# Gate and up projections of a feed-forward stage by one level of Strassen's algorithm

## The chip, the cores and the metric

The kernel runs on one core of one Trainium2 chip. The metric is device time in microseconds (us) of one execution; the kernel before took 2920.21 us (median of 3 runs, 2919.99 to 2921.68). Engines are named as in the profile: PE multiplies matrices (PEld is its loading of stationary operands), DVE and ACT work on vectors, POOL does small things, SP issues all DMAs of this kernel, in one queue that goes in order.

## The reference

One layer of a hybrid network over 16 learned tokens and 2048 tokens of width 1024 in float32: a token mixer (a state space model and a chunked mLSTM, merged by gates, then a projection and a norm), and behind it the channel mixer, which the change is about:

```python
def channel_mixer(x, g_pre, g_post, w_gate, w_up, w_conv, b_conv, w_down):
    h = rmsnorm(x, g_pre)
    a = causal_dwconv(h @ w_gate, w_conv, b_conv)      # 3 taps over the tokens
    y = (jax.nn.gelu(a, approximate=True) * (h @ w_up)) @ w_down
    return x + rmsnorm(y, g_post)
```

w_gate and w_up are 1024 × 2816, w_down is 2816 × 1024. The first 16 tokens give no output; of them only the last two matter here, for the convolution.

## The kernel before

Every float32 product is made of three matmuls in a reduced type: an operand is split into a high part (a copy by ACT, rounded to that type) and a low part (operand minus high part, by DVE), and `mm3` (lines 145 to 148) adds high × high, high × low and low × high. So an operand that is made on the chip costs one operation of ACT and one of DVE beside what makes it.

The order of the instructions on each engine is not written by hand. The program states them in its own order, and a planner sorts them at compile time: on each engine it takes, of what is ready by its own estimate of times, what the program states first. On the chip each engine then keeps that order. A tile of a pool has a tag and a number of buffers; the next tile of a tag waits until the buffer that it takes is no longer read. A pool that is opened where another was closed waits, tile by tile, for those that lay at its place. PSUM has two buffers of tag "mm", four of "ac" and two of "tp", a bank each.

Stages up to line 829 (projections, state space model, mLSTM) are the same in both kernels. What follows:

- Phase C (lines 831 to 1065) goes over four blocks of 512 tokens (the first has 514, with the two tokens ahead). For each block `front_a` and `front_b` fetch the two branches' inputs, `glu` gates the first, `branches` projects and merges both into `mh`, `ml` (high and low part, from pool `cr`), `out_proj` multiplies by `w_out` in two halves of its columns, loading each 128 × 512 slice when it is due, and `out_post` applies the norm and the residual and stores `h1_d` in DRAM. `out_post` of a block is stated behind `branches` of the next one; that of block 3 comes last. Operand tiles `t4(i)` are 128 × 4 × 514 in size; the tags t0 to t7 are in use.
- `norm_tile` (lines 107 to 125) loads 128 tokens of `h1_d`, takes the sum of squares (ACT), the factor (DVE, POOL), scales by it and by the row `g_ffn_pre` (DVE, line 114), transposes by PE (line 120), and splits from PSUM into the FFN's operands (ACT line 124, DVE line 125). Blocks 0 and 1 are done during the last block of phase C into t0 to t7, blocks 2 and 3 at the beginning of the next stage into the tiles q0 to q7.
- The gate and up stage goes over 22 slices m of 128 columns of `w_gate` and `w_up`. `load_w` (lines 137 to 143) fetches each slice of 128 × 1024 and splits it. `ffn_unit` (lines 1090 to 1116) then does a block of tokens: 24 matmuls for gate into "ac" (48 in block 0, whose 514 columns are cut at 258 and 256), a copy to `gp_` (ACT, line 1099), the convolution (ACT line 1106, two taps on DVE line 1108), the function gelu (ACT line 1109), 24 matmuls for up into "mm", the product (DVE, line 1115) and the store to `y_d` (line 1116). All four blocks' operands lie on the chip, so each weight is loaded and split once. The last two columns of a block's gate are kept in `halo` (POOL, lines 1101 and 1104).
- The down stage (lines 1136 to 1183) loads `w_down` in two halves of columns and splits it into t0 to t7 and q0 to q2, and goes twice over 16 tiles of tokens: load `y_d` (line 1160), split (lines 1163 and 1164), 66 matmuls, and the norm and the residual at the end of the second half.

## Time and profile before

| | |
|---|---|
| time, median of 3 runs | 2920.21 us (2919.99 to 2921.68) |
| span of the profiled execution, first to last instruction | 2927.4 us |
| mean granted clock of PE | 0.997 |
| PE busy, matmuls | 2883.3 us (98%), 14862 |
| PEld, loads of stationary operands | 2529.4 us (86%) |
| DVE, ACT, POOL busy | 1346.9 us (46%), 898.9 us (31%), 153.8 us (5%) |
| gate and up stage, first matmul to the down stage | 1444.2 to 2429 us |
| bytes read from and written to DRAM | 244.08 MB, 95.72 MB |

The profiled execution has no separate time of its own beside its span; the span is 7.2 us longer than the median of the runs, which were not profiled. Lines are those of the kernel's file; a helper's line stands for all its callers, so `mm3`'s lines 146 to 148 hold nearly all matmuls, and their output and input tiles tell the stages apart: "ac<-t,wh" and "mm<-q,wh" are the gate and up stage, "ac<-t,yh" the down stage. In rows of groups the numbers are the busy time, the mean length of one in ns, and the idle time of the engine just ahead, with what ended it. In the order of time a row begins with its start and its length; "x2" merges two. Neighbouring instructions of an engine overlap a little in the records, so the cost of one in a row of many is the step from start to start.

### The profile page before, as it was taken

Reading aid. Unit: us, or ns where it says so; the run is one execution under the profiler, and the core shown is the slowest. Engines: PE = TensorE matmul, PEld = TensorE weight load, DVE = VectorE, ACT = ScalarE, POOL = GpSimd, SP = SyncE. Lnnn points to the kernel's source line nnn. Section 1 sums busy time; section 2 is a strip of 40 time slices with the busy share of each in tenths; the row PEclk is TensorE's granted clock in tenths of the full one; section 3 lists DMA queues with packets and bytes.
Section 4 is the critical chain, followed back from the end, with each engine's and each line's share of the span. In section 5 each row is a group of like instructions: output and inputs, shape, how many; then the busy total and the mean of one; then the engine's idle time right before and its main releaser. Section 6 shows DMA issues by size and latency. Waiting matters only on the chain.

```text
span 2927.4 us, 38298 instructions
## 1 busy us (share of the span) xinstructions
PE 2883.3 (98%) x14862; PEld 2529.4 (86%) x14862; DVE 1346.9 (46%) x2617; ACT 898.9 (31%) x1683; POOL 153.8 (5%) x331
## 2 busy tenths in 40 slices
PE   9999999999999999999999999999999999999999
PEld 8999999999999987777788888888888888887887
DVE  4638897377554546566652222222222233224333
ACT  6102232233443435435342222222222232223221
POOL 1000000000000000320310000000000000000000
PEclk9999999999999999999999999999999999999999
DMA  9334453222553655665631111111111134334654
GB/s 298 103 73 139 164 168 114 69 69 71 163 154 119 198 169 159 188 207 165 202 109 44 54 40 51 55 46 54 48 43 54 44 107 126 97 99 145 184 165 124
DMA packets 299848, 342.32 MB, mean 117 GB/s; under 512 B 38849, under 2 KB 208470, under 8 KB 299538
## 3 DMA queue, kind: packets, MB, share of 16 engines
q1 hardware_dynamic: 299666, 339.88, 37.9%
q8 instruction: 116, 1.90, 0.3%
q14 instruction: 66, 0.54, 0.1%
HBM read 244.08 MB, written 95.72 MB: 116 GB/s over the span
## 4 chain that ended last, share of the span: by engine, by line
PE 86%; DMA 5%; DVE 3%; issue 3%; ACT 1%; POOL 1%; SPq 0%; POOLq 0%; DVEq 0%; ACTq 0%
PE mm L146 14%; PE mm L148 14%; PE mm L147 14%; PE ac L146 13%; PE ac L148 13%; PE ac L147 13%; DMA xt<-in_x_dram 1%; DMA wo_d<-W 1%; POOL o L1003 1%; DMA ws<-in_w_out_dram 1%; DMA xs<-in_h_t_dram 1%; PE ac L484 0%; PE ac L482 0%; PE ac L457 0%; PE ac L388 0%
## 5 line engine op out<-in xcount | busy, mean ns | idle before, releaser
L148 PE MATMUL mm<-hTh,wl 128*128 128x410 f32 (+3 forms) x1216 | 430.3, 354 | 0.0
L146 PE MATMUL mm<-hTh,wh 128*128 128x410 f32 (+3 forms) x1216 | 429.6, 353 | 0.2 <-DVE ev L336 0.2
L147 PE MATMUL mm<-hTl,wh 128*128 128x410 f32 (+3 forms) x1216 | 426.7, 351 | 0.0
L130 ACT ACTIVATE wh<-ws 128x512 fp32r<-128x512 f32 (+1 forms) x220 | 171.4, 779 | 478.3 <-PE mm L147 152.4
L1108 DVE SCALAR_TENSOR_TENSOR cc<-gp,cw,cc 128x512 f32<-128x512 f32 x176 | 132.3, 752 | 353.1 <-ACT cc L1106 350.1
L132 DVE TENSOR_TENSOR wl<-ws,wh 128x512 fp32r<-128x512 f32 (+1 forms) x156 | 157.8, 1012 | 243.6 <-ACT wh L130 241.2
L1164 DVE TENSOR_TENSOR yl<-ys,yh 128x1408 fp32r<-128x1408 f32 x64 | 104.0, 1626 | 304.2 <-ACT yh L1163 304.2
L146 PEld LDWEIGHTS mm<-hTh,wh 128*128 128x128 f32 x1216 | 229.4, 189 | 2.9 <-DVE ev L336 0.7
L148 PEld LDWEIGHTS mm<-hTh,wl 128*128 128x128 f32 x1216 | 229.4, 189 | 2.5
L147 PEld LDWEIGHTS mm<-hTl,wh 128*128 128x128 f32 x1216 | 229.4, 189 | 2.1
L147 PE MATMUL ac<-t,wh 128*128 128x512 f32 (+2 forms) x688 | 223.1, 326 | 0.0
L148 PE MATMUL ac<-t,wl 128*128 128x512 f32 (+2 forms) x688 | 220.8, 327 | 1.6 <-DVE wl L134 1.6
L146 PE MATMUL ac<-t,wh 128*128 128x512 f32 (+2 forms) x688 | 222.2, 327 | 0.0
L146 PE MATMUL mm<-t,wh 128*128 128x512 f32 (+2 forms) x544 | 208.1, 383 | 1.8 <-ACT wh L130 1.8
L148 PE MATMUL mm<-t,wl 128*128 128x512 f32 (+2 forms) x544 | 207.1, 383 | 0.7 <-DVE wl L134 0.7
L147 PE MATMUL mm<-t,wh 128*128 128x512 f32 (+2 forms) x544 | 207.2, 381 | 0.0
L146 PE MATMUL ac<-t,yh 128*128 128x512 f32 x512 | 201.8, 394 | 1.4 <-ACT t L1154 0.8
L148 PE MATMUL ac<-t,yl 128*128 128x512 f32 x512 | 202.1, 395 | 0.2 <-DVE yl L1164 0.2
L147 PE MATMUL ac<-t,yh 128*128 128x512 f32 x512 | 202.1, 395 | 0.0
L1163 ACT ACTIVATE yh<-ys 128x1408 fp32r<-128x1408 f32 x64 | 88.4, 1381 | 349.0 <-PE ac L147 347.4
L1099 ACT ACTIVATE gp<-ac 128x512 f32<-128x512 f32 (+2 forms) x110 | 56.0, 510 | 389.9 <-PE ac L148 389.7
L1115 DVE TENSOR_TENSOR cc<-cc,mm 128x512 f32<-128x512 f32 x88 | 60.5, 688 | 189.9 <-PE mm L148 189.7
(425 smaller groups left out, 5806.1 us busy)
## 6 DMA issues: line engine op xcount, KB each, us to landing
ys<-y_d SPq DMA_DIRECT2D x64, 704.0 KB, 4.9
y_d<-cc SPq DMA_DIRECT2D x88, 256.0 KB, 2.0
gab_d<-ev SPq DMA_DIRECT2D x80, 205.0 KB, 2.5
ws<-in_w_m_dram SPq DMA_DIRECT2D x32, 512.0 KB, 3.9
ws<-in_w_out_dram SPq DMA_DIRECT2D x64, 256.0 KB, 3.4
gat<-gab_d SPq DMA_DIRECT2D x48, 256.0 KB, 3.5
ws<-in_w_gate_dram SPq DMA_DIRECT2D x22, 512.0 KB, 3.7
ws<-in_w_up_dram SPq DMA_DIRECT2D x22, 512.0 KB, 3.8
```

The costliest lines, as they stand in the source:

```text
L130: S.activation(wh, ws, AF.Copy, scale=scale)
L132: V.tensor_tensor(wl, ws, wh.bitcast(F32), ALU.subtract)
L146: T.matmul(out=ps, lhsT=lh, rhs=rh, start=first, stop=False)
L147: T.matmul(out=ps, lhsT=lh, rhs=rl, start=False, stop=False)
L148: T.matmul(out=ps, lhsT=ll, rhs=rh, start=False, stop=last)
L1003: (V if b == 3 else G).tensor_tensor(o[:rows], o[:rows], xt[:rows], ALU.add)
L1099: S.activation(gp_[:, o:o + pn], ps, AF.Copy)
L1108: V.scalar_tensor_tensor(c, gp_[:, j:j + 512], cw[:, m, j:j + 1], c, ALU.mult, ALU.add)
L1115: V.tensor_tensor(c, c, pu, ALU.mult)
L1163: S.activation(yh, ys, AF.Copy)
L1164: V.tensor_tensor(yl, ys, yh.bitcast(F32), ALU.subtract)
```

## The change

The gate and up stage becomes a block product: the weights are a 2 × 2 matrix A of blocks (rows gate and up, columns the two halves of the 1024 input features), the normed input is a 2 × 2 matrix B (rows the halves of the features, columns two stretches of tokens). Strassen's algorithm (in Winograd's form) makes the four blocks of A·B from 7 block products instead of 8, with sums of blocks as operands. Two passes over all 22 slices are made: pass 0 over the first 1026 tokens (two stretches of 514 columns, the first beginning with two columns of zeros; each product is cut into 258 and 256 columns), pass 1 over the other 1024 (512 each, not cut). Weights are loaded, summed and split in each pass (`ffn_weights`), with one copy per product.

In `ffn_unit` three PSUM banks A, B, C take the products in the order 1, 6, 2, 7, 5, 4, 3 (A: 1, 2; B: 6, 7, 4; C: 5, 3); a bank is added to by a later product after the sum so far has been read (`mm3x`). Copies to `u1` and of gate's first half are ACT's, the five other sums are DVE's.

The operands from the input are sums too, so `norm_tile` now stores the transposed, normed input as `h2_d` in DRAM (scaled there by `g3`, a column of g_ffn_pre), and `op_load` reads it back, a quarter of a pass at a time, for `ops_first` (operands of products 1, 6, 2, 7) and `ops_second` (5, 4, 3). Their tiles are t0 to t11 and q0, q1, which hold one pass. `ops_first(0)` is stated ahead of `out_post` of block 3, `ops_second(0)` behind it; the norms of blocks 2 and 3 are stated behind slice 1 of pass 0, and the operands of pass 1 between the passes.

To make room, `mh` and `ml` of phase C move to t8 to t11, a pool `mk` of three tiles replaces those of `front_a`, and serves the norm, `op_load` and at the end two of the down stage's tiles. The down stage's pool `el` is opened at the place of `dx`, the gate and up stage's pool, after that is closed; w_down's slices and two small tiles use buffers of the weights' pool `dw`. Removed comments are left out below.

```diff
+    h2_d = dp.tile([128, KD, L], F32, name="h2_d")
...
+    g3 = const.tile([128, KD], F32, name="g3")
+    P.dma_start(out=g3, in_=g_ffn_pre)
+
+    def norm_tile(t, pl, t0, rows):
+
+        xt, hs = t[:, 0:D], t[:, D:2 * D]
+        P.dma_start(out=xt[:rows], in_=h1_d[t0:t0 + rows, :])
         ssq = pl.tile([128, 1], F32, tag="ssq", name="ssq")
         S.activation(hs[:rows], xt[:rows], AF.Square, accum_out=ssq[:rows])
         rs = rstd_of(pl, ssq, rows, 1, 1.0 / D)
-        V.scalar_tensor_tensor(hs[:rows], xt[:rows], rs[:rows], g_b[:rows], ALU.mult, ALU.mult)
+        V.tensor_scalar(hs[:rows], xt[:rows], rs[:rows], None, ALU.mult)
+        hr = xt.rearrange("p (k t) -> p k t", k=KD)
...
-            for j in range(0, per, 4):
-                dh = dst_h[(q * per + j) // 4][:, :, c0:c0 + rows]
-                dl = dst_l[(q * per + j) // 4][:, :, c0:c0 + rows]
-                S.activation(dh, tp[:, j:j + 4], AF.Copy)
-                V.tensor_tensor(dl, tp[:, j:j + 4], dh.bitcast(F32), ALU.subtract)
+            ks = slice(q * per, q * per + per)
+            V.tensor_tensor(hr[:, ks, :rows], tp, g3[:, ks].unsqueeze(2).to_broadcast([128, per, rows]), ALU.mult)
+        P.dma_start(out=h2_d[:, :, t0:t0 + rows], in_=hr[:, :, :rows])
...
+    def mk_tile(dt=F32):
+        return mk.tile([128, 4 * 520], dt, tag="mk", name="mk", bufs=3)
...
-        mh = cr.tile([128, KD, 514], F32R, tag="mh", name="mh")
-        ml = cr.tile([128, KD, 514], F32R, tag="ml", name="ml")
+        mh, ml = [t4(8), t4(9)], [t4(10), t4(11)]
...
+    WX = (514, 512)
+
+    def op_load(p, hf, half):
+        w = WX[p]
+        t = mk_tile()[:, 0:4 * w].rearrange("p (k c) -> p k c", k=2)
+        ks = slice(4 * half + 2 * hf, 4 * half + 2 * hf + 2)
+        if p == 0:
+            G.memset(t[:, :, 0:2], 0.0)
+            P.dma_start(out=t[:, :, 2:2 * w], in_=h2_d[:, ks, 14:14 + 2 * w - 2])
+        else:
+            P.dma_start(out=t, in_=h2_d[:, ks, 1040:1040 + 2 * w])
+        return t[:, :, 0:w], t[:, :, w:2 * w]
+
+    def op_split(op, p, hf, src):
+        hi, lo = (o[:, 2 * hf:2 * hf + 2, 0:WX[p]] for o in op)
+        S.activation(hi, src, AF.Copy)
+        V.tensor_tensor(lo, src, hi.bitcast(F32), ALU.subtract)
+
+    def ops_first(p):
+
+        op = {n: (t4(2 * i), t4(2 * i + 1)) for i, n in enumerate((1, 6, 2, 7))}
+        for hf in range(2):
+            b11, b12 = op_load(p, hf, 0)
+            op_split(op[1], p, hf, b11)
+            b21, b22 = op_load(p, hf, 1)
+            V.tensor_tensor(b11, b12, b11, ALU.subtract)
+            V.tensor_tensor(b12, b22, b12, ALU.subtract)
+            V.tensor_tensor(b22, b22, b11, ALU.subtract)
+            op_split(op[6], p, hf, b22)
+            op_split(op[2], p, hf, b21)
+            op_split(op[7], p, hf, b12)
+        return op
+
+    def ops_second(p, op, last):
+
+        op.update({5: (t4(8), t4(9)), 4: (t4(10), t4(11)), 3: last()})
+        for hf in range(2):
+            b11, b12 = op_load(p, hf, 0)
+            b21, b22 = op_load(p, hf, 1)
+            V.tensor_tensor(b11, b12, b11, ALU.subtract)
+            op_split(op[5], p, hf, b11)
+            V.tensor_tensor(b12, b22, b11, ALU.subtract)
+            V.tensor_tensor(b21, b21, b12, ALU.subtract)
+            op_split(op[4], p, hf, b21)
+            op_split(op[3], p, hf, b22)
...
+    op0 = ops_first(0)
     for f in posts(3):
         f()
     phC.close()
...
+        def put(n, pl, tag, src):
+            t = pl.tile([128, 2, 512], F32R, tag=tag, name=f"w{n}")
+            S.activation(t[:, 0], src, AF.Copy)
+            V.tensor_tensor(t[:, 1], src, t[:, 0].bitcast(F32), ALU.subtract)
+            out_[n] = t.rearrange("p a (k f) -> p a k f", k=4)
...
+        put(1, dw, "wh", a11)
+        V.tensor_tensor(s1, a21, a22, ALU.add)
+        V.tensor_tensor(s2, s1, a11, ALU.subtract)
+        put(6, dw, "wh", s2)
+        put(2, dw, "wl", a12)
+        V.tensor_tensor(s3, a11, a21, ALU.subtract)
+        put(7, dw, "wl", s3)
+        put(5, dx, "w5", s1)
+        put(4, dx, "w4", a22)
+        s4 = dx.tile([128, 512], F32, tag="s3", name="s4")
+        V.tensor_tensor(s4, a12, s2, ALU.subtract)
+        put(3, dx, "w3", s4)
+        return out_
...
+    def ffn_unit(p, m, op):
+        wt = ffn_weights(m)
+        w = WX[p]
+        gp_ = dx.tile([128, 1028], F32, tag="gp", name="gp")
...
+        for p0, pn in (((0, 258), (258, 256)) if p == 0 else ((0, 512),)):
+
+            def prod(ps, n, first):
+                for k in range(4):
+                    mm3x(ps, wt[n][:, 0, k], wt[n][:, 1, k], op[n][0][:, k, p0:p0 + pn], op[n][1][:, k, p0:p0 + pn],
+                         first and k == 0, k == 3)
...
+            A, B, C = pst("ac", [128, pn]), pst("mm", [128, pn]), pst("ac", [128, pn])
+            u1, u2, u3 = acc("u1", 2), acc("u2", 1), acc("u3", 2)
+            prod(A, 1, True)
+            S.activation(u1, A, AF.Copy)
+            prod(B, 6, True)
+            V.tensor_tensor(u2, B, u1, ALU.add)
+            prod(A, 2, False)
+            S.activation(gp_[:, x0 + p0:x0 + p0 + pn], A, AF.Copy)
+            prod(B, 7, False)
+            V.tensor_tensor(u3, B, u1, ALU.add)
+            prod(C, 5, True)
+            V.tensor_tensor(u3, C, u3, ALU.add)
+            prod(B, 4, False)
+            V.tensor_tensor(u1, B, u1, ALU.add)
+            prod(C, 3, False)
+            V.tensor_tensor(gp_[:, x0 + w + p0:x0 + w + p0 + pn], C, u2, ALU.add)
...
+    ops_second(0, op0, lambda: (q4(0), q4(1)))
+    for m in range(NF):
+        ffn_unit(0, m, op0)
+        if m == 1:
+            norm_block(2, dsm)
+            norm_block(3, dsm)
+    op1 = ops_first(1)
+    ops_second(1, op1, lambda: (q4(0), q4(1)))
+    for m in range(NF):
+        ffn_unit(1, m, op1)
+    phX.close()
     el = pool(ctx, "el", bufs=2)
...
-            w_s = el.tile([128, 2, 512], F32, tag="wds", name="wds")
+            w_s = dw.tile([128, 2, 512], F32, tag="wh", name="wds")
```

The rest of the new `ffn_unit` is the convolution, gelu, product and store as before, in two parts of some 512 tokens.

More of the change, by code (lines that the diff above doesn't have):

```diff
@@ L1073, in q4 @@
     def q4(i):
[L1074 to L1081 removed]
+        return hq.tile([128, 4, 514], F32R, tag=f"q{i}", name=f"q{i}")
+    phX = ExitStack()
+    dx = pool(phX, "dx")
+    dsm = Small(dx, "n", 2)
```

158 lines of the change are left out of this document (62 added, 96 removed).

## The prediction

> **What bounds the kernel now.** I read the page's shares first, then the stretches around the stage that changes, then that stage's instructions in order of time.
>
> ```profile
> PE 2883.3 (98%) x14862; PEld 2529.4 (86%) x14862; DVE 1346.9 (46%) x2617; ACT 898.9 (31%) x1683; POOL 153.8 (5%) x331
> PE 86%; DMA 5%; DVE 3%; issue 3%; ACT 1%; POOL 1%; SPq 0%; POOLq 0%; DVEq 0%; ACTq 0%
> ```
>
> PE is busy 98% of the span and holds 86% of the chain that ended last. A busy PE can hide slow matmuls, so the windows come next (after the stretch and its length: PE, PEld, DVE, ACT, POOL busy with their counts, granted clock, DMA share, GB/s).
>
> ```profile
> core 0: us, PE busy (x) PEld busy (x) DVE busy (x) ACT busy (x) POOL busy (x), PEclk, DMA share, GB/s
> 1390.00:1444.00 54.00, 49.34 (x221) 38.80 (x220) 28.93 (x47) 18.74 (x33) 16.33 (x12) 1.00 0.61 190
> 1444.00:1463.00 19.00, 19.00 (x106) 16.49 (x105) 15.33 (x31) 8.78 (x22) 5.63 (x6) 1.00 0.71 231
> 1463.00:1503.00 40.00, 40.00 (x222) 34.15 (x221) 27.46 (x39) 23.10 (x41) 6.45 (x14) 1.00 0.43 148
> 1503.00:2430.00 927.00, 925.93 (x4495) 777.05 (x4494) 249.41 (x317) 229.32 (x335) 24.00 (x124) 1.00 0.18 57
> ```
>
> The gate and up stage runs from 1444 to 2430. PE waits about 1 us in it, at full clock, and DVE works 27% of the time: the stage is as long as its matmuls. Its period per slice m is the distance between two loads of a gate weight; the pitch of matmuls comes from their starts.
>
> ```profile
> 1893.69 0.33 SPq L139 DMA_DIRECT2D ws<-in_w_gate_dram  x1
> 1938.07 0.33 SPq L139 DMA_DIRECT2D ws<-in_w_gate_dram  x1
> 1982.45 0.33 SPq L139 DMA_DIRECT2D ws<-in_w_gate_dram  x1
> ...
> 1444.23 0.28 PE L146 MATMUL ac<-t,wh 128*128 128x258 f32 x1
> 1445.91 0.28 PE L148 MATMUL ac<-t,wl 128*128 128x258 f32 x1
> ...
> 1599.81 0.39 PE L147 MATMUL ac<-t,wh 128*128 128x512 f32 x1
> 1608.38 0.39 PE L148 MATMUL mm<-t,wl 128*128 128x512 f32 x1
> ```
>
> A slice takes 44.38 us: 48 matmuls of 258 or 256 columns and 168 of 512. The 14 steps from 1444.23 to 1445.91 give 0.120 us for 258 columns; I use 0.119 for the mean of 258 and 256. The 37 steps from 1599.81 to 1608.38 give 0.2316 us for 512. Two half-width matmuls cost 0.238, 3% more than one full one.
>
> **The matmuls removed.** For 1024 tokens a slice had 8 products of 4 k tiles (gate and up, two halves of k, two halves of the tokens); now it has 7, each with 4 × 3 = 12 matmuls. Pass 0 cuts all of them at 258 and 256 columns: 168 × 0.119 = 20.0 us. Pass 1 keeps 512: 84 × 0.2316 = 19.45 us. 22 × 39.45 = 868 us against 22 × 44.38 = 976.4: **−108.5 us**. PE needs no further instruction: the transposes of the norm were there before.
>
> **What a slice now asks of DVE and ACT.** The nearest rows:
>
> ```profile
> 1394.85 0.69 DVE L951 TENSOR_TENSOR gat<-gat 128x512 f32<-128x512 f32 x1
> 1395.45 0.69 DVE L132 TENSOR_TENSOR wl<-ws,wh 128x512 fp32r<-128x512 f32 x1
> ...
> 1893.83 1.54 DVE L1108 SCALAR_TENSOR_TENSOR cc<-gp,cw,cc 128x512 f32<-128x512 f32 x2 [0.16 <-ACT cc L1106]
> ...
> L393 DVE TENSOR_TENSOR a<-ac,cc x32: 404/422/430, 334.1 to 488.1; 128x258 f32<-128x258 f32 x32
> ...
> L130 ACT ACTIVATE wh<-ws 128x512 fp32r<-128x512 f32 x78 | 49.3, 632 | 100.8 <-DMA ws<-in_w_out_dram 54.5 <-PE ac L148 22.6 <-DMA ws<-in_w_a_dram 7.5
> L1099 ACT ACTIVATE gp<-ac 128x258 f32<-128x258 f32 x22 | 8.5, 385 | 52.2 <-PE ac L148 52.2
> L1106 ACT ACTIVATE cc<-gp,cb,cw 128x512 f32<-128x512 f32 x88 | 71.8, 816 | 6.1 <-issue 0.4
> L1109 ACT ACTIVATE cc<-cc 128x512 f32<-128x512 f32 x88 | 55.6, 632 | 136.0 <-DVE cc L1108 136.0
> ```
>
> Back to back, a 512-wide two-input operation costs DVE 0.60 us (0.69 long, the next one starts 0.09 before its end); one of 258 from PSUM 0.42 − 0.09 = 0.33; a pair of convolution taps 1.54. Per slice and pass the weights ask for 11 subtractions and additions, since both passes split them anew: 6.6 us. Pass 0 adds 10 sums out of PSUM (3.3), two pairs of taps (3.1) and four products with up (1.3): 14.3 of 20.0 us. Pass 1: 6.6 + 5 × 0.60 + 3.1 + 2 × 0.60 = 13.9 of 19.45. ACT has at most 7 × 0.63 + 4 × 0.39 + 2 × 0.82 + 2 × 0.63 = 8.9 us. So DVE goes from 27% to some 72%: on average it stays behind PE. The 1 MB of weights per slice and pass fits into 20 us (512 KB land in 3.7 us, a row quoted further down).
>
> The **new wait** is inside a slice: the second product into bank A, the second and third into B and the second into C add to a sum that ACT or DVE must have read first, with one other product between. That product lasts 12 × 0.119 = 1.43 us in pass 0 and 2.78 in pass 1.
>
> ```profile
> 1900.09 0.40 PE L148 MATMUL ac<-t,wl 128*128 128x258 f32 x2
> 1900.40 0.39 ACT L1099 ACTIVATE gp<-ac 128x258 f32<-128x258 f32 x1 [2.51 <-PE ac L148]
> ```
>
> The second of these two matmuls starts near 1900.21 and its slot ends at 1900.33; ACT starts 0.07 later. With 0.42 for the reading, 0.5 of 1.43 us is used, so one tap (0.77) ahead in DVE's queue still fits and a pair does not. The taps of slice m−1 and leftovers of the weights of m stand ahead of the sums of m only near a slice's start. Bounds: 0, and 22 slices × 8 reuses × 0.2 = 35. I take 0.3 us a slice: **+7**. Pass 1 has twice the room: 0. The weights have one copy per product, but copy n is free once product n of the last piece is done and is wanted six products (8.6 us) later, against 0.63 + 0.69 for its split: 0 while DVE keeps up.
>
> **Where the operands are made.** Operand tiles are now sums over h2, read back from DRAM: 8 loads of 1 MB per pass through three buffers, 14 operations of 1028 elements on DVE for products 1, 6, 2, 7 and 12 for 5, 4, 3.
>
> ```profile
> 1447.48 1.22 DVE L132 TENSOR_TENSOR wl<-ws,wh 128x1024 fp32r<-128x1024 f32 x1
> 1448.62 0.15 DVE L991 TENSOR_TENSOR sq<-ssq 128x1 f32<-128x1 f32 x1
> ...
> ys<-y_d SPq DMA_DIRECT2D x64, 704.0 KB, 4.9
> xt<-h_d SPq DMA_DIRECT2D x16, 512.0 KB, 4.2
> ws<-in_w_gate_dram SPq DMA_DIRECT2D x22, 512.0 KB, 3.7
> ...
> L1002 DVE SCALAR_TENSOR_TENSOR o<-o,rs,g2b 128x512 f32<-128x512 f32 x24 | 16.9, 747 | 6.6 <-POOL rs L104 6.5
> L1003 DVE TENSOR_TENSOR o<-o,x 128x512 f32<-128x512 f32 x8 | 5.1, 684 | 0.0
> ...
> PE ac L147 <- DVE wl L132: 6.2, 7, 1.8
> ```
>
> One such operation costs 1.14 us; a 1 MB load, extended from 4.2 and 4.9 us, about 6.
>
> *Ahead of the stage* (1390 to 1444): the norms of blocks 0 and 1 now also store h2, and ops_first's four loads come behind them on SP, in front of w_out slices. DVE is 54% busy there and takes the 16 us. But PE already waits 4.7 of 54 us (the last row above names its longest wait of this kind, for w_out's splits), and 7 MB more makes 190 GB/s into some 320. **+5** (0 to 12).
>
> *Start of pass 0*: the operands of 5 and 4 take the tiles that the out projection reads until 1444, and those of 3 take space held by out_post. Behind that moment stand on DVE out_post (8 × 0.75 + 8 × 0.68 = 11 us), ops_second (12 × 1.14 = 13.7), what the weights of slice 0 could not do earlier, as w_out held their buffers (4.6), and the slice's own sums (3.3): 32.6 us against 20.0 of matmuls. PE can begin with products 1 and 6, then waits; out_post's waits for POOL and the last loads are added. **+20**; from 4 (out_post made late) to 32 (everything in turn).
>
> *Norms of blocks 2 and 3*, in the slices behind: they took 40 us before (1463 to 1503) without holding PE. They ask DVE for about as much as then, 2.0 to 2.8 us a tile, some 20 in all, but beside 72% instead of 27%: 0.72 × 40 + 20 = 49 us of work in 40. **+6** (0 to 12), as the weights have slack.
>
> *Between the passes*: the tile of product 1 is free 8.6 us ahead of the pass's end. From there DVE owes the end of slice 21 (6 us), 26 × 1.14 = 29.6 of operands, 6.6 of weights and 3 of sums: 45 us, while PE would need 8.6 + 19.45 = 28. Five of the eight loads wait for a buffer, two in turn at 6 us each, which ends at about the same time. **+19** (8 to 30).
>
> *Start of the down stage*: its first tiles ran into the stage before without a gap (PE 10.00 of 10.00 around 2430); the ys tiles were loaded long ahead. Now ys, yh, yl lie where the last slice's weights, gp and sums lie, so the first yh and yl (1.38 and 1.63 us) follow the last tap. **+6** (2 to 12).
>
> ```profile
> 2430.00:2440.00 10.00, 10.00 (x45) 8.08 (x44) 4.80 (x6) 3.17 (x4) 0.00 (x0) 1.00 0.41 133
> L1163 ACT ACTIVATE yh<-ys 128x1408 fp32r<-128x1408 f32 x64 | 88.4, 1381 | 349.0 <-PE ac L147 347.4
> L1164 DVE TENSOR_TENSOR yl<-ys,yh 128x1408 fp32r<-128x1408 f32 x64 | 104.0, 1626 | 304.2 <-ACT yh L1163 304.2
> ```
>
> **The sum**: −108.5 + 5 + 20 + 6 + 7 + 19 + 6 = −45.5. The profiled span is 2927.4 us, so 2881.9 there; the runs' median, 2920.2, lies 7.2 below the span, and I carry that over: **2875 us**.
>
> **The rivals.**
> *A, the sum above*, 2850 to 2900: 0.48.
>
> ```profile
> 1896.98 0.28 PE L147 MATMUL ac<-t,wh 128*128 128x258 f32 x1
> 1897.10 0.28 PE L146 MATMUL ac<-t,wh 128*128 128x256 f32 x1
> ...
> 1897.34 0.39 PE L146 MATMUL ac<-t,wh 128*128 128x512 f32 x1
> ```
>
> *B, the seams are hidden*: the planner puts operand work into DVE's free time and pulls matmuls of other pieces forward, as in these rows, where 258-, 256- and 512-wide matmuls alternate. Seams of 2 + 6 + 2 + 2 + 9 + 3 = 24 us: 2836. For it: DVE is idle 46% ahead of the stage. Against it: tiles that PE still reads. 0.17.
> *C, DVE paces pass 0*: 1.5 us a slice instead of 0.3: 2901. For it: 72% on average is more in a slice's second half, where weights and taps meet. 0.19.
> *D, slower*: the sums come back late at every reuse in pass 0. DVE runs in a fixed order; if the planner sets a pair of taps or two weight splits ahead of the sums, each reuse takes 0.07 + 1.54 + 0.42 − 1.43 = 0.6 us too long, 8 × 0.6 × 22 = 106 us: 2875 − 7 + 106 = 2974. It makes the change a loss from (45.5 + 7) / 176 = 0.30 us a reuse. Against it: a pair must stand there each time. 0.13.
> *E, slower: short matmuls do not hide the weight loads.* The stage now has 22 × 252 = 5544 loads against 4752.
>
> ```profile
> L146 PEld LDWEIGHTS ac<-t,wh 128*128 128x128 f32 x688 | 129.5, 188 | 12.8 <-ACT wh L130 0.4
> ```
>
> 792 more loads at 0.188 us, all bare, are 149 us: 3024. The pitch of 0.119, less than the 0.188 of one load, says that they overlap at 258 columns too: 0.02. [...]
> The last 0.01 is for no saving at all: the same sums would have to be multiplied anyway, which the product count excludes.
>
> **How the numbers follow.** A measurement of this kernel tells a change of 0.2%, 5.8 us, from none. A and B are faster (0.65); C spreads over 2888 to 2920 and is faster for 0.17 of its 0.19, with 0.02 within 0.2%; of D 0.10 is slower, 0.02 within and 0.01 faster; E is slower, the rest within. Faster 0.83, same 0.05, slower 0.12. The range goes from just below B's time to C's end, 2832 to 2920, and leaves out B's lower part, D and E.
>
> **What would show it.** Right: mean pitches of 0.119 and 0.232 us in the two passes, 252 matmuls a slice; PE idle in three clusters (behind the out projection, between the passes, ahead of the down stage) of 20, 19 and 6 us; DVE 70 to 75% busy in between with PE gapless; slices of 20 and 19.5 us. Wrong: PE waits on the sums' DVE lines spread over all slices of pass 0 (C, D), PE waits on weight splits, or clusters under 10 us (B).

## The result and the profile after

The changed kernel takes 2949.02 us (median of 4 runs, 2948.23 to 2950.64) against 2920.51 us of the kernel before (4 runs, 2919.99 to 2921.68): ratio 1.0093, 95% interval 1.0078 to 1.0107. It is 0.9% slower, where 2875 us and faster had been forecast. The saving in matmuls came nearly as forecast, and the seams and the late sums took more than all of it.

The page of the changed kernel, its busy times and its granted clock:

```profile
PE 2811.1 (95%) x15654; PEld 2512.8 (85%) x15654; DVE 1786.0 (61%) x3482; ACT 1041.7 (35%) x1963; POOL 155.6 (5%) x251
...
PE   8999999999999999999689999989999988999999
```

The profiled execution spans 2948.8 us (2927.4 before). PE went from 98% to 95% of a longer span, and in the row of slices its idle time stands in clusters. Stretches cut at those places (columns as in the prediction: stretch and length; PE, PEld, DVE, ACT, POOL busy with counts; clock; DMA share; GB/s):

```profile
1390.00:1454.00 64.00, 55.15 (x216) 43.19 (x217) 39.28 (x53) 24.15 (x37) 16.86 (x16) 0.92 0.71 242
1454.00:1480.00 26.00, 5.30 (x30) 5.05 (x29) 25.04 (x40) 11.99 (x26) 6.62 (x5) 0.63 0.45 146
1480.00:1550.00 70.00, 62.89 (x496) 61.00 (x494) 51.16 (x101) 27.85 (x52) 7.26 (x10) 0.97 0.52 161
1550.00:1965.00 415.00, 388.51 (x3180) 382.61 (x3180) 290.49 (x557) 162.05 (x287) 4.47 (x19) 1.00 0.24 82
1965.00:2007.00 42.00, 33.37 (x143) 25.83 (x143) 39.60 (x56) 20.12 (x28) 6.83 (x2) 0.84 0.47 169
2007.00:2424.00 417.00, 412.55 (x1766) 332.98 (x1765) 297.80 (x472) 173.24 (x281) 13.62 (x21) 1.00 0.28 89
2424.00:2444.00 20.00, 0.00 (x0) 0.00 (x0) 9.61 (x15) 8.20 (x13) 0.00 (x0) 0.57 0.81 237
2444.00:2456.00 12.00, 11.36 (x36) 8.60 (x37) 3.25 (x2) 2.18 (x3) 0.00 (x0) 0.72 0.65 199
```

Pass 0 runs from 1454 to 1965. In its steady part (1550 to 1965) PE is idle 26.5 of 415 us, while DVE is 70% busy: not the average load, but its order. In pass 1 (2007 to 2424) PE is idle 4.5 of 417 us. DVE is busy for nearly all of both operand seams (25.0 of 26 us; 39.6 of 42). Ahead of the down stage PE does nothing for 20 us, where the kernel before had no gap. What PE waited for, in four stretches: the start of pass 0, its steady part, the start of the down stage, and the end of phase C (us in total, times, longest):

```profile
PE ac L154 <- ACT u L1179: 20.7, 1, 20.7
...
PE mm L154 <- DVE u L1185: 19.4, 18, 1.6
...
PE ac L149 <- ACT yh L1253: 20.2, 1, 20.2
PE mm L154 <- DVE u L1185: 3.0, 1, 3.0
...
PE ac L150 <- DVE wl L135: 7.2, 2, 4.0
```

The second row is new in kind: the same sum, u3 = B + u1 (line 1185), is late in 18 of some 20 slices, by 1 us each. Where it is late, DVE (left to right: start, length, operation) and then PE:

```profile
1721.93 0.69 DVE L1139 TENSOR_TENSOR s<-wu 128x512 f32<-128x512 f32 x1 [0.36 <-DMA wu<-in_w_up_dram]
1722.54 0.68 DVE L1143 TENSOR_TENSOR s<-wg,wu 128x512 f32<-128x512 f32 x1
1723.14 0.75 DVE L1206 TENSOR_TENSOR cc<-cc,u 128x258 f32<-128x258 f32 x2
1723.81 0.68 DVE L1140 TENSOR_TENSOR s<-s,wg 128x512 f32<-128x512 f32 x1
1724.41 0.74 DVE L1201 SCALAR_TENSOR_TENSOR cc<-gp,cw,cc 128x510 f32<-128x510 f32 x1
1725.07 0.42 DVE L1185 TENSOR_TENSOR u<-mm,u 128x258 f32<-128x258 f32 x1
```

```profile
1725.54 0.39 PE L154 MATMUL mm<-t,w 128*128 128x258 f32 x1 [1.43 <-DVE u L1185]
```

Three sums of the next slice's weights (lines 1139, 1143, 1140), two products with up and one tap stand ahead of the 0.42 us that PE needs. They take 3.1 us together. The first of them waits 0.36 us for w_up's slice, and what stands behind it in DVE's order waits too. PE waits 1.43 us. The order was fixed at compile time, and in the trace the same six operations stand ahead of this sum in all 18 cases.

### The profile page after: what moved, and what is told of

It reads as the page before. It is cut to its first block, busy times and chain, and to the rows that moved or that the text cites. A ratio compares the mean times of both kernels' runs of the same rounds, so it can differ in the third digit from the quotient of the medians.

```text
span 2948.8 us, 41275 instructions
## 1 busy us (share of the span) xinstructions
PE 2811.1 (95%) x15654; PEld 2512.8 (85%) x15654; DVE 1786.0 (61%) x3482; ACT 1041.7 (35%) x1963; POOL 155.6 (5%) x251
## 5 line engine op out<-in xcount | busy, mean ns | idle before, releaser
L149 PE MATMUL ac<-t,yh 128*128 128x512 f32 x704 | 278.9, 396 | 21.9 <-ACT yh L1253 20.7
L154 PE MATMUL ac<-t,w 128*128 128x256 f32 (+2 forms) x792 | 258.8, 327 | 37.4 <-ACT u L1179 21.6
L154 PE MATMUL mm<-t,w 128*128 128x258 f32 (+2 forms) x792 | 255.1, 325 | 25.8 <-DVE u L1185 22.6
L151 PE MATMUL ac<-t,yl 128*128 128x512 f32 x704 | 278.9, 397 | 0.5 <-DVE yl L1254 0.4
L150 PE MATMUL ac<-t,yh 128*128 128x512 f32 x704 | 278.7, 396 | 0.0
L155 PE MATMUL ac<-t,w 128*128 128x256 f32 (+2 forms) x792 | 256.8, 324 | 0.0
L156 PE MATMUL ac<-t,w 128*128 128x258 f32 (+2 forms) x792 | 254.9, 324 | 1.4 <-DVE w L1132 1.4
L155 PE MATMUL mm<-t,w 128*128 128x258 f32 (+2 forms) x792 | 254.1, 321 | 1.3 <-DVE t L1041 1.3
L156 PE MATMUL mm<-t,w 128*128 128x258 f32 (+2 forms) x792 | 253.7, 320 | 0.0
L133 ACT ACTIVATE wh<-ws 128x512 fp32r<-128x512 f32 (+1 forms) x176 | 124.7, 708 | 321.4 <-PE mm L150 140.2
L154 PEld LDWEIGHTS ac<-t,w 128*128 128x128 f32 x792 | 152.2, 192 | 54.0 <-ACT u L1179 23.3
L1131 ACT ACTIVATE w<-s 128x512 fp32r<-128x512 f32 x176 | 110.3, 628 | 230.4 <-PE mm L156 109.6
L154 PEld LDWEIGHTS mm<-t,w 128*128 128x128 f32 x792 | 150.1, 190 | 44.0 <-DVE u L1185 24.2
L149 PEld LDWEIGHTS ac<-t,yh 128*128 128x128 f32 x704 | 133.5, 190 | 54.9 <-ACT yh L1253 21.6
```

Of the source, the lines that this page charges most:

```text
L133: S.activation(wh, ws, AF.Copy, scale=scale)
L149: T.matmul(out=ps, lhsT=lh, rhs=rh, start=first, stop=False)
L150: T.matmul(out=ps, lhsT=lh, rhs=rl, start=False, stop=False)
L151: T.matmul(out=ps, lhsT=ll, rhs=rh, start=False, stop=last)
L154: T.matmul(out=ps, lhsT=lh, rhs=rh, start=first, stop=False, skip_group_check=True)
L155: T.matmul(out=ps, lhsT=lh, rhs=rl, start=False, stop=False, skip_group_check=True)
```

## The experiments

Experiments e1 to e8 ran once each, beside one run of the kernel before on the same chip (2921.1 us), and e9 to e11 beside one of 2925.1 us on another chip, so a few us between the two groups say nothing; e12 to e14 have four runs each, beside seven. "Unit" is the distance between the first matmuls of two slices (the expectation of e11_spread counts units from 0); a gap is counted from the start of the last matmul ahead of it to the start of the next. The changed kernel has units of 45.8, 29.8 and 27.4 us, then 21.2 to 22.5 in pass 0, and 42.5, then 19.5 in pass 1.

**1. Whose sums are late in pass 0.** e1_pool moves the four sums of the weights to POOL (GpSimd; VectorE is DVE and ScalarE is ACT):

```diff
-        V.tensor_tensor(s1, a21, a22, ALU.add)
+        G.tensor_tensor(s1, a21, a22, ALU.add)
... (the same for s2, s3, s4)
```

> The four sums of weight blocks (s1, s2, s3, s4) go from DVE to POOL; all else as in the changed kernel. Theory 1: in pass 0 PE loses 1.3 us a slice because the sum u3 stands on DVE behind the weight sums of the next slice, which all become ready when the up weights land, and behind taps. Then a slice of pass 0 goes from 21.5 to 20.3 to 20.7 us, and the kernel from 2949 to 2920 to 2932. Rival: the taps alone hold u3, or the longer half-width products are the cause; then a slice stays at 21.3 to 21.5 us and the time within 5 us of 2949.

2955.74 us. From the fifth on, units of pass 0 fell to 20.1 to 21.7 us. The wait on the same line (1560 to 1950) fell from 18 times to 8. The second row is one of the moved sums in the groups of instructions (busy us, mean ns):

```profile
PE mm L154 <- DVE u L1185: 3.6, 8, 1.2
```

```profile
L1140 POOL TENSOR_TENSOR s<-s,wg 128x512 f32<-128x512 f32 x44 | 74.4, 1691 | 0.0
```

So the weights' sums did stand in the way. But the four sums cost 1.4 to 1.7 us each on POOL, the weights come later, and pass 1 went from 19.5 to 20.3 us per slice: pass 0 shrank by 14.6 us, pass 1 grew by 17.8, and the time by 6.7.

e4_inter takes the other side, and gives DVE more time. The two pieces of pass 0 take turns product by product, so that two products instead of one lie between the writing of a sum and its bank's next use:

```diff
-        for p0, pn in (((0, 258), (258, 256)) if p == 0 else ((0, 512),)):
...
-            prod(A, 1, True)
-            S.activation(u1, A, AF.Copy)
-            prod(B, 6, True)
-            V.tensor_tensor(u2, B, u1, ALU.add)
...
+        for q in Q:
+            prod(q, A[q], 1, True)
+            S.activation(u1[q], A[q], AF.Copy)
+        for q in Q:
+            prod(q, B[q], 6, True)
+            V.tensor_tensor(u2[q], B[q], u1[q], ALU.add)
...
```

> In pass 0 the two pieces of a slice take turns: product 1 of both, then product 6 of both, and so on; u2 gets a second buffer. The instructions of every engine are the same in number and size. Theory 1: a bank is then added to again two products (2.86 us) after its last one, not one (1.43 us), and the sums have the room to wait behind weights and taps: slices of pass 0 go from 21.5 to 20.2 us and the time falls by 20 to 28 us, to 2921 to 2929. Rival: DVE has too much to do in pass 0 in all, and any order of products loses the same; then slices stay at 21.3 us or more.

2908.78 us, 40 us less than the changed kernel (20 to 28 were expected), and already below the kernel before. The steady part, and two starts of a slice (the loads of its gate weights) in this kernel and then in the changed one:

```profile
1556.00:1929.00 373.00, 373.00 (x3118) 372.95 (x3117) 285.77 (x544) 158.12 (x281) 3.31 (x18) 1.00 0.27 90
```

```profile
1747.64 0.33 SPq L1123 DMA_DIRECT2D wg<-in_w_gate_dram  x1
1767.74 0.33 SPq L1123 DMA_DIRECT2D wg<-in_w_gate_dram  x1
```

```profile
1737.06 0.33 SPq L1123 DMA_DIRECT2D wg<-in_w_gate_dram  x1
1758.32 0.33 SPq L1123 DMA_DIRECT2D wg<-in_w_gate_dram  x1
```

PE is busy 373.00 of 373.00 us with DVE at 77%; a slice takes 20.10 us instead of 21.3. The instructions are the same in number and size (u2 alone has a second buffer, as two pieces are open at once), so the loss was in the distance to the next use of a bank, not in how much DVE has to do. Pass 0 shrank from 510.6 to 468.5 us.

**2. The start of the down stage.** e2_tables moves the small tables (`cw`, `cb`, `halo`) out of the pool that the down stage's tiles lie over. e3_first, on top of that, gives the first half of the first tile of y (ys, yh, yl) buffers of the operand loads:

```diff
-    cb = dx.tile([128, NF], F32, name="cb")
+    cbf = const.tile([128, NF], F32, name="cbf")
```

```diff
-                ys = el.tile([128, 11, 128], F32, tag="ys", name="ys")
+                early = nh == 0 and i == 0 and kh == 0
+                ys = first[0] if early else el.tile([128, 11, 128], F32, tag="ys", name="ys")
... (yh and yl likewise, first = three tiles of the operand loads)
```

> The tables of the convolution (cw, cb) and halo, 528 bytes a partition at the lowest places of pool dx, move to the constants; all else as in the changed kernel. Theory 2: the 20.2 us without matmuls ahead of the down stage come from where pool el lies: its first ys buffer covers cb, which ACT reads until the last slice's convolution, and ys then stands in SP's queue behind the last store. With the tables gone the first ys waits only for weight sums and lands before the last slice ends; the gap shrinks to some 10 us, where yl waits for the space of gp and u1, and the time falls by 10 to 15 us, to 2934 to 2939. Rival: w_down's slices or the order of SP's queue set the start, whatever el covers; then the gap stays within 2 us of 20.

> As the run with the tables moved, and the first half of the down stage's first tile (ys, yh, yl) lies in the three buffers of pool mk, which are free since pass 1 began. Theory 2: PE then has 33 matmuls (7.6 us) right behind the last slice, and the rest of the wait is for the second half's yl; the gap is 0 to 5 us in all, no stretch at half clock follows, and the time falls by 22 to 29 us against the changed kernel, to 2920 to 2927. Rival as above: w_down's slices come too late, and the gap is as in the run with the tables alone.

2959.82 and 2949.81 us. The gap stayed at 20.0 and 22.1 us; the places of tables and of one half tile are not what PE waits for. (e2_tables lost 10.8 us, none of them in this gap: its trace is 2.9 us late at the start of pass 0, 3.9 longer in pass 0 and 5.0 in pass 1; the cause is open.) In e3_first the early half's 33 matmuls did run ahead, inside the last slice, but the second half's loads went out at 2443.6 us, behind the last store at 2439.0. SP's queue in the changed kernel:

```profile
2429.30 2.92 SPq L1239 DMA_DIRECT2D wds<-in_w_down_dram  x2
2432.64 0.34 SPq L1207 DMA_DIRECT2D y_d<-cc  x1
2435.01 0.37 SPq L1239 DMA_DIRECT2D wds<-in_w_down_dram  x1
2435.43 1.21 SPq L1250 DMA_DIRECT2D ys<-y_d  x2
```

Loads of w_down (`wds`) are still going out when the up stage is over, each waiting for one of two staging buffers, and the loads of y stand behind them. e5_wds uses four buffers on e4_inter; e6_both adds e3_first's early half tile, with the tables left in place; e9_seam gives both halves of the first tile's loads buffers of their own instead, with e2_tables' edit and the split copies placed over buffers that come free first:

```diff
-            w_s = dw.tile([128, 2, 512], F32, tag="wh", name="wds")
+            w_s = dw.tile([128, 2, 512], F32, tag="wh" if nh or k % 4 else "ws", name="wds")
```

Of e9_seam:

```diff
-                ys = el.tile([128, 11, 128], F32, tag="ys", name="ys")
+                early = nh == 0 and i == 0
+                ys = first[kh] if early else el.tile([128, 11, 128], F32, tag="ys", name="ys")
...
-                yh = el.tile([128, 11, 128], F32R, tag="yh", name="yh")
                 yl = el.tile([128, 11, 128], F32R, tag="yl", name="yl")
+                yh = el.tile([128, 11, 128], F32R, tag="yh", name="yh")
```

> Pass 0 with its two pieces taking turns (as in e4_inter, 2908.8 us), and beside it the slices of w_down of the down stage's first half staged through four buffers instead of two (every other slice through the buffers of w_gate and w_up, which are free during the last slice of the up stage). In e4_inter the last matmul of the up stage ends at 2380.9 us and the first of the down stage starts at 2402.4, a gap of 21.6 us; the eleven slices are issued from 2357 to 2396 us, one per 3.5 us, each waiting for a buffer. Theory (the two staging buffers pace the start of the down stage): eleven slices at about 2 us each end by about 2383; the first tile of y, 6.4 us to land and 1.4 us to split, then sets the start; the gap falls to 8 to 14 us and the time to 2896 to 2903 us. Rival (the first tile of y is loaded only behind the last store of the up stage, issued at 2390.2 in the order of SP's queue): the gap stays at 17 us or more and the time at 2904 to 2909 us.

> As e5_wds, and the first half of the first tile of y loaded and split in the free buffers of the operand loads, so that it waits for no buffer of the up stage. Theory (both the slices of w_down and the first tile of y are late, one behind the other): the gap of 21.6 us falls to 2 to 7 us and the time to 2889 to 2896 us, 5 us or more below e5_wds. Rival (one of the two was the whole cause): within 2 us of e5_wds, either with a gap that is small in both, or large in both.

> As e5_wds (2906.5 us, up stage's last matmul at 2382.0, down stage's first at 2400.0), and three places more: the small tables are kept in the pool of constants, the first tile of y (both halves) is loaded into the free buffers of the operand loads instead of buffers that lie over the up stage's tiles, and the split copies of y lie over buffers that come free early in the last slice. Theory (in e5_wds the first tile's loads, issued at 2392.7 us behind the last store at 2392.2, 5.5 us to land and 1.4 us to split, set the start; loads into buffers of their own are issued long before): the gap of 18 us falls to 2 to 6 us; time 2890 to 2896 us. Rival (as in e6_both, the down stage's early work is taken into the last slice and delays it, on ScalarE and VectorE, by as much as is won): the up stage's last matmul comes 5 us or more later and the time stays at 2902 us or more.

e5_wds: 2906.46 us, gap 18.0 instead of 21.6. The loads of w_down were through, and the next thing was late, as the rival said (SP's queue, and ACT):

```profile
2379.88 2.09 SPq L1247 DMA_DIRECT2D wds<-in_w_down_dram  x2
...
2389.43 3.16 SPq L1215 DMA_DIRECT2D y_d<-cc  x2
2392.68 1.24 SPq L1258 DMA_DIRECT2D ys<-y_d  x2
```

```profile
2398.57 1.38 ACT L1261 ACTIVATE yh<-ys 128x1408 fp32r<-128x1408 f32 x1 [7.06 <-DMA ys<-y_d]
```

The last store is issued at 2392.2 (the second of the two), the loads of y behind it, and 5.9 us later they have landed. e6_both missed: 2914.73 us. The up stage's last matmuls came 14.7 us later in it; the 33 early ones are 7.6 us of this, and the rest was not lost in the last slice. It lies in the middle of pass 1, whose slices took 20.1 us on average instead of 19.5, with PE waiting 14 times for a weight's split (line 1132, 1975 to 2360 us); why is open. The gap remained 18.8 us for the second half. e9_seam: 2904.04 us, gap 9.3 us, 8.7 less than in e5_wds where 12 to 16 were expected. Of this the time shows only 2.4 us (2890 to 2896 had been expected), since pass 0 began 4.8 us later and its first unit took 47.2 us instead of 43.9, ahead of the seam. Now ACT's order is last:

```profile
2395.80 1.15 ACT L1252 ACTIVATE t<-wds 128x512 fp32r<-128x512 f32 x2 [3.32 <-DMA wds<-in_w_down_dram]
...
2398.38 2.63 ACT L1265 ACTIVATE yh<-mk 128x1408 fp32r<-128x1408 f32 x2
```

So three things were late one behind the other: w_down through two buffers, the loads of y behind the last store in SP's queue, and the split of y behind w_down's last split on ACT.

**3. The start of pass 0.** e7_pool moves the last block's residual sums and the second operand set's sums to GpSimd, e8_late states the first operand set behind the last block's norms, and e10_early states slice 0's weight sums ahead of them and puts u1 and u2 over buffers that are free early (all on e4_inter):

```diff
-            (V if b == 3 else G).tensor_tensor(o[:rows], o[:rows], xt[:rows], ALU.add)
+            G.tensor_tensor(o[:rows], o[:rows], xt[:rows], ALU.add)
... (in ops_second, V to G in the three sums)
```

```diff
-    op0 = ops_first(0)
     for f in posts(3):
         f()
+    op0 = ops_first(0)
```

```diff
     op0 = ops_first(0)
+    ts0 = mk_tile()
+    w0 = weights_first(0, [ts0[:, 512 * j:512 * j + 512] for j in range(3)])
     for f in posts(3):
         f()
... (weights_first: the part of ffn_weights for products 1, 6, 2, 7; u1, u2, gp allocated first)
```

> As e4_inter, with two things moved from VectorE to GpSimd: the eight residual sums of the last block of the mixer (0.68 us each on VectorE at 1467 to 1481) and the six sums of the second operand set of each pass (1.22 us each). Theory (at the start of pass 0 and between the passes the order of VectorE's work sets the gap): VectorE has 12 us less to do in the first place and 7 us less in the second; the start gap of 19.3 us falls to 10 to 14 us, the first unit from 43.7 to 33 to 37 us, the first unit of pass 1 from 41.3 to 34 to 37; time 2893 to 2900 us. Rival (GpSimd, 1.5 us for 128x512 and about 3 us for 128x1028, is late with the same sums, and the buffers that they hold come free later): gaps as before or longer, 2904 to 2915 us.

> As e4_inter, with the first operand set of pass 0 made after the last block of the mixer is normed instead of before it. The stage ahead ended its matmuls at 1444.0 us in the kernel before, and at 1453.9 to 1459.9 us in the changed kernels. Theory (the operand loads and splits under the last output projection lengthen that stage): its last matmul comes at 1443 to 1449 us; the gap after it grows to 30 us or more, as the operands are now made in it; 2905 to 2916 us. Rival (the stage is longer for another reason, such as the weights' loads for the first slice or the place of buffers): its last matmul stays at 1454 us or later, and the time rises to 2915 to 2925 us.

> As e4_inter (2908.8 us; start gap 19.3 us, first unit 43.7 us), with two things at the start of pass 0: the sums of the first slice's weights are made in a buffer of the operand loads, ahead of the last block's residual sums in VectorE's order, and the accumulators u1 and u2 lie over buffers that are free before those sums, not over the norm's gain and the projection's copies. Theory (the start gap is VectorE's order plus the place of the accumulators): the copy of the first product no longer waits until 1481.7 us, products of the first unit run under the residual sums, and the first unit falls from 43.7 to 33 to 38 us; time 2897 to 2904 us. Rival (VectorE's work there is the bound in sum, whatever its order): the single gap of 19.3 us breaks up into several, the first four units together (112.4 us in e4_inter) shrink by less than 3 us, time 2905 to 2910 us.

e7_pool: 2919.25 us, a miss; the start gap grew from 19.3 to 26.3 us. POOL has the operand sums (line 1067) and the residual sums (line 1014) in one order, ACT stands 16.8 us for an operand sum, and the copy to u1, for which PE waits, follows behind three more copies in ACT's order (POOL, ACT, PE's wait):

```profile
1476.84 2.48 POOL L1014 TENSOR_TENSOR o<-o,x 128x512 f32<-128x512 f32 x2
...
1479.79 2.01 POOL L1067 TENSOR_TENSOR mk<-mk 128x1028 f32<-128x1028 f32 x1
```

```profile
1481.83 1.06 ACT L1040 ACTIVATE t<-mk 128x1028 fp32r<-128x1028 f32 x1 [16.78 <-POOL mk L1067]
...
1485.54 0.64 ACT L1182 ACTIVATE u<-ac 128x258 f32<-128x258 f32 x2
```

```profile
PE ac L154 <- ACT u L1182: 26.0, 1, 26.0
```

In e4_inter ACT stands 9.5 us for the same sum, on DVE there, ahead of the same copies. So the gap ends with operand work in a fixed order; whether u1's place, over the last block's tiles, had set that order is not shown by these rows. e10_early takes that place away, and the rival held in the units, though the gap did not break up: 2904.29 us, PE runs 7.3 us before its gap instead of 2.8, but the gap is 20.6 us, and the first four units take 114.7 us against 112.4. PE now waits for the copy of product 5's weights, which ACT makes behind an operand copy that stands 8.1 us for DVE's sum, and this sum waits 2.6 us for its load. DVE is busy 25.7 of the 30 us from 1451 to 1481, so its order can win little there; less work for DVE was tried only in e7_pool. What e10_early won, it won ahead: phase C's last matmul came at 1450.8 us instead of 1459.9. e8_late, 2914.70 us, told nothing of its question: the planner issued the operand loads at the same place as before, between w_out's slices, and phase C's last matmul came at 1464.7.

**4. The norms of blocks 2 and 3.** e11_spread makes one norm tile per slice, from slice 1 to 8:

```diff
-        if m == 1:
-            norm_block(2, dsm)
-            norm_block(3, dsm)
+        if 1 <= m <= 8:
+            b, i = 2 + (m - 1) // 4, (m - 1) % 4
+            norm_tile(mk_tile(), dsm, blkC[b][0] + blkC[b][3][i][0], 128)
```

> As e4_inter, with the eight norm tiles of the last two token blocks made one to a slice from slice 1 to slice 8, instead of all together behind slice 1. Units 1 to 3 of pass 0 take 20.9, 24.1 and 23.7 us in e4_inter and 20.1 from the fifth on; the transposes of a tile are 16 short matmuls, some 0.9 us on TensorE. Theory (bunched norm tiles overload VectorE and ScalarE there): units 1 to 8 take 20.5 to 21.3 us each, their sum falls by 1 to 3 us; time 2905 to 2908 us. Rival (the units are long since VectorE works off the first unit's backlog): units 2 and 3 stay at 23 us or more; time 2908 to 2913 us.

2909.77 us. Slices with a tile take 20.9 to 21.0 us, those without 20.1: 0.9 us a tile, about the length of its eight transposes on PE (0.80 us in the changed kernel, 1493.21 to the next matmul at 1494.01). The first ten units shrank by 2.2 us in sum, as the theory had it; phase C's end was 3.4 us later and hid it in the time.

**5. All of it, and the clock.** e12_all puts e4_inter, e9_seam, e11_spread and the early weight sums of e10_early together. e13_fill_start and e14_fill_down add to it matmuls whose sums nothing reads, to keep PE from idling:

```diff
+        if p == 0 and m == 0:
+            fill(70, op[1][0], tail[0])
```

```diff
+    fill(36, op1[3][0], tail[0])
     phX.close()
     el = pool(ctx, "el", bufs=2)
```

> All of it together: the two pieces of pass 0 taking turns (e4_inter), the down stage's start as in e9_seam, the first slice's weight sums ahead of the last block's residual sums (as e10_early, with the accumulators left where they were), and the norm tiles one to a slice (as e11_spread). Theory (the gains add up where they concern different places: 7 us at the start of the down stage from e9_seam against e4_inter, and 2 us of norm tiles from e11_spread; the start of pass 0 stays bound by VectorE's work): 2893 to 2902 us, so 0.991 to 0.994 of the kernel before. Rival (the wander of the mixer's last stage, whose last matmul has come anywhere from 1450.8 to 1464.7 us with the order of VectorE's work, decides): 2902 to 2912 us, with that matmul at 1460 us or later.

> As e12_all (2892.5 us), with 70 matmuls of 512 columns (0.232 us each at full clock, 16 us) put into the start gap of pass 0 (20.9 us from 1459.1 us in e12_all); they read an operand and nothing reads their sums. In e12_all the clock is at half for 20.5 us from 1475.2 us. Theory (the half clock comes from TensorE standing idle): the stretch at half clock disappears or shrinks below 7 us. If TensorE's speed there counts, the first unit falls from 44.7 us by 4 to 8 us and the time to 2884 to 2889 us. Rival (VectorE's work is the bound in the first units, so that slow matmuls cost nothing there): the stretch disappears, and unit and time stay within 2 us.

> As e12_all, with 36 such matmuls (8.3 us) put into the gap between the up and the down stage (11.3 us from 2378.1 us in e12_all). There the clock is at half for 6.8 us from 2379.7 and 13.7 us from 2393.4 us, and TensorE is busy in the second of them. Theory (idle TensorE brings the half clock, and in the down stage nothing but TensorE is late): both stretches disappear or shrink below 7 us together, matmuls in 2390 to 2407 take 0.232 us instead of 0.43, and the time falls by 4 to 7 us to 2885 to 2889 us. Rival (the half clock comes some 20 us after a change of load whatever TensorE does in the gap): the second stretch stays, time within 2 us of e12_all.

e12_all: 2892.54 us against 2922.73, ratio 0.9893 (0.9876 to 0.9909): faster than both kernels. The two others: ratios 0.9881 (0.9861 to 0.9901) and 0.9874 (0.9857 to 0.9891). Neither can be told from e12_all. The stretches at the start of pass 0, e12_all and then e13_fill_start (the clock stands behind POOL's count):

```profile
1459.00:1467.00 8.00, 0.41 (x4) 0.20 (x2) 7.56 (x13) 0.00 (x0) 4.01 (x3) 0.82 0.35 131
1467.00:1475.00 8.00, 0.00 (x0) 0.00 (x0) 5.85 (x8) 1.06 (x1) 2.55 (x2) 0.50 0.53 140
1475.00:1483.00 8.00, 2.99 (x14) 2.99 (x15) 6.59 (x9) 4.74 (x8) 0.10 (x1) 0.50 0.67 210
```

```profile
1456.00:1464.00 8.00, 8.00 (x37) 6.60 (x37) 7.56 (x15) 0.00 (x0) 4.14 (x2) 1.00 0.30 113
1464.00:1472.00 8.00, 6.88 (x42) 6.00 (x40) 6.23 (x10) 1.07 (x1) 2.65 (x2) 1.00 0.53 138
1472.00:1480.00 8.00, 2.34 (x11) 2.34 (x12) 5.95 (x8) 4.74 (x8) 0.10 (x1) 0.75 0.65 217
```

The times of the half clock in the last two expectations are some 11 us too late against these rows: in e12_all the clock falls near 1464 us (0.82 in 1459 to 1467, 0.50 in the two stretches behind), 5 us into PE's gap and not 16. While the fill runs, the clock stays at 1.00; the first unit is 45.3 us against 44.7. Slow matmuls cost nothing there, since PE waits for DVE anyway (the rival). At the down stage the fill had run out 3.3 us before the first tile came, and the clock is low again (0.72, the row below): the first 81 matmuls of the stage take 22.2 us against 22.3 in e12_all. What no idling at all would give there stays open. e14_fill_down, the stretch around the first tile:

```profile
2378.00:2390.00 12.00, 8.45 (x25) 5.98 (x24) 7.17 (x8) 4.94 (x7) 0.00 (x0) 0.72 0.79 221
```

## Why the prediction was wrong

The terms, each measured in the traces of the two kernels. The base is 976.4 us. The stage took 985.2 us before, from its first matmul (1444.2) to that of the down stage (2429.4); the 8.8 us above the base are transposes and waits, and they are taken off the row "norms".

| term | forecast, us | measured, us |
|---|---|---|
| matmuls | −108.5 | −104.5 |
| phase C, blocks 2 and 3 | +5 (0 to 12) | +15.5 |
| start of pass 0 | +20 (4 to 32) | +25.7 |
| norms | +6 (0 to 12) | +8.2 |
| late sums in pass 0 | +7 (0 to 35) | +25.7 |
| between the passes | +19 (8 to 30) | +23.0 |
| start of the down stage | +6 (2 to 12) | +33.4 |
| sum | −45.5 | +27.0 |

The measured terms are worked out so: pass 0 lasts 510.6 us (first matmul 1454.2, that of pass 1 1964.8) against 22 × 20.1 = 442.2; the first three units are above 20.1 by 25.7, 9.7 and 7.3 (the last two less 8.8: norms), the other 19 by 25.7 together. Pass 1's first unit is 23.0 above 19.53. From the last matmul of block 1's output projection to that of block 3's, phase C takes 240.2 us (1213.7 to 1453.9) instead of 224.7 (1219.3 to 1444.0). Start of the down stage: pass 1 lasts 479.4 us to the down stage's first matmul (2444.2), 26.7 more than 22 × 19.53 and the 23.0, and the stage itself takes 497.7 us from its first matmul to its last instead of 491.0.

The medians differ by 28.5 us, the two traces by 21.4 only. In every run that has both, the span is 1.7 to 1.9 us below the run's time, so the execution that the trace of the kernel before shows (2927.4 us) took some 9 us more than the median. Of the 7.1 us between the two differences 5.6 lie ahead of blocks 2 and 3, in work that is nearly the same in both kernels (1219.3 against 1213.7; the changed kernels themselves lie between 1211.4 and 1220.3 there). The table leaves this out: its 27.0 less 5.6 is the difference of the traces, and 1.5 us of the 28.5 are left over. The 7.2 us between span and median, which the prediction carried over, belong to this execution and are not added by profiling.

**Right.** The count and the pitch: 20.1 and 19.53 us a slice when nothing is late (forecast 20.0 and 19.45), so short matmuls do hide their weight loads, and rival E fell. The trace of before had this in it (loads of 0.188 us at the same pitch of 0.119), and the trace of the changed kernel shows it again: a load in the stage lasts 0.192 us, longer than the pitch of 0.119 (the groups of the changed kernel; busy us, mean ns, idle us before). What lets them overlap, no run shows.

```profile
L154 PEld LDWEIGHTS ac<-t,w 128*128 128x128 f32 x792 | 152.2, 192 | 54.0 <-ACT u L1179 23.3
```

Right also: pass 1 without gaps, DVE at 70% in between, the seam between the passes filled with DVE's work (39.6 of 42 us), and three clusters of idle PE.

**Wrong by the order of a fixed queue: the late sums (+7, measured 25.7).** The step that failed is "the taps of slice m−1 and leftovers of the weights of m stand ahead of the sums of m only near a slice's start", and with it 0.3 us a slice. The runs showed 1.35 us a slice in the changed kernel: weight sums of the *next* slice stand in mid slice, ahead of the same bank reuse each time. That is rival C's size (1.5 us a slice) with rival D's mechanism at one reuse in eight. The forecast had the right number for the room (1.43 us a product) and the right queue (DVE in fixed order), and then took an average of 72% as if work came evenly. e4_inter, which doubles the room and leaves the work alone, settles it.

**Wrong in kind: the start of the down stage (+6, measured 33.4).** The step that failed priced only the first split, "the first yh and yl (1.38 and 1.63 us) follow the last tap". What takes part besides: eleven slices of w_down that can be split only when the last slice's operands are done (before, their tiles came free block by block over the last slice's 44 us, and the first tile of y had buffers of its own), two staging buffers for them, loads of y that SP issues behind the last store, and ACT's order. e5_wds and e9_seam took one off after the other: gaps of 21.6, 18.0 and 9.3 us. In the kernel before, the loads of the first tile of y went out 29 us ahead of its first matmul (2429.4); that this lead needs space *and* queue places, was not followed through:

```profile
2400.30 1.73 SPq L1160 DMA_DIRECT2D ys<-y_d  x2
```

**Sizes.** The start of pass 0 (+20, measured 25.7) has the named mechanism; e10_early's order did not help it, and in e7_pool moving sums to POOL made it worse. In the norms (+6, measured 8.2) the transposes have no part, since the kernel before had them too: 0.9 us a tile, which e11_spread leaves. The rest is mostly work left over from the first unit, not the norms' own: in e4_inter the second to fourth units are 8.4 us above 20.1 in sum, as much as the 8.8 before (the second falls from 29.8 to 20.9 us once pieces take turns), and e11_spread takes some 2 us of that away. Between the passes (+19, measured 23.0) nothing was separated: e7_pool took sums off DVE there too, and pass 1's first unit was 42.2 us against 41.3 in e4_inter, but POOL's sums are slower (2.0 to 2.9 us for 128 × 1028 in e7_pool, 1.22 on DVE in e4_inter).

**Phase C (+5, measured 15.5)** lies outside its range and is half open. PE idles 19.3 us in blocks 2 and 3 instead of 10.0, and is busy 220.9 us instead of 214.7 for as many matmuls (938 and 939 records). An estimated 4 of these 6.2 us are a term that the prediction put at nothing, slow matmuls: from 1418.4 to 1423.1 the clock is 0.50, and a matmul of 512 columns takes 0.427 us instead of 0.232; 31 of them step by 0.38 to 0.45 us in the two blocks, 11 did before, and 20 more at 0.2 us are 4. PE waits for w_out's splits, 3.19 and 4.01 us. The first wait, what DVE did, and what POOL did meanwhile:

```profile
1409.21 0.50 PE L150 MATMUL ac<-wl,t 128*128 128x512 f32 x1 [3.19 <-DVE wl L135]
```

```profile
1395.19 0.68 DVE L135 TENSOR_TENSOR wl<-ws,wh 128x512 fp32r<-128x512 f32 x1
...
1405.23 2.24 DVE L1052 TENSOR_TENSOR mk<-mk 128x1028 f32<-128x1028 f32 x1
1407.39 1.76 DVE L135 TENSOR_TENSOR wl<-ws,wh 128x512 fp32r<-128x512 f32 x1
```

```profile
1404.67 3.94 POOL L1014 TENSOR_TENSOR o<-o,xh 128x512 f32<-128x512 f32 x2 [2.21 <-DVE o L1013]
1408.57 0.99 POOL L105 TENSOR_TENSOR rs<-ms,neghalf 128x1 f32<-128x1 f32 x1
```

An operand sum stands ahead of w_out's split, and both are slow. That this order makes the idle time was not isolated: e8_late missed it. Blocks 2 and 3, measured as above, take 239.9 to 245.3 us in the changed kernels, and 233.3 to 237.1 in the four that state slice 0's weight sums early; why these are shorter was not tried either.

## What to carry to other kernels

A fast algorithm that saves multiplications puts sums between them, and each sum between two uses of an accumulator is a deadline on an engine with a fixed queue: price it by the longest run of work that can stand ahead of it, not by that engine's average load, and make the deadline longer (two pieces taking turns) before making the work shorter. At a seam, list everything that the next stage had prepared under the old one (its weights, its staging buffers, its loads' places in the queue, its first split); taking the space away makes all of it late, one behind the other, and each repair shows the next.

## What the runs showed of the hardware

*DVE was slower beside POOL's additions.* In the rows above a split of 128 × 512 takes 0.68 us alone and 1.76 while POOL adds two tiles, and a sum of 1028 elements 2.24, where the sum just ahead of it (line 1051, at 1402.69, POOL idle) took 1.23. Ten us later, beside POOL's next two additions (1413.32 to 1417.23), an operand's split of 1028 elements takes 2.22 (line 1041, at 1413.89) and the one ahead of it 1.21. POOL's own addition of 128 × 512 takes 1.2 to 2.0 us in e7_pool and here, against 0.68 on DVE. What makes DVE slower there, no run shows. Work is thus not moved off DVE for nothing, which e1_pool and e7_pool show in their times (6.7 us more than the changed kernel, 10.5 more than e4_inter).

*What the half clock costs.* PE's granted clock is 0.63 in the first 26 us of pass 0 and 0.57 in the gap ahead of the down stage, but most of that time PE is idle. The 12 us after that gap hold 36 matmuls, 8.3 us at the pitch of 0.2316 and the clock of 1.00, so slow matmuls and short waits cost 3.7 us at most there. In phase C (0.92 from 1390 to 1454) it falls on matmuls that PE needs, at 0.427 us each, and the estimate above gives it some 4 of the 15.5 us.
